# Score products of the first block: two of 128 rows in place of three of 64

## Chip, core and metric

The kernel is one program on one core of a Trainium2 chip. The metric is the device time of one execution in microseconds (us); the time before is the median of three executions.

## What is computed

Two transformer blocks follow each other. The change is in the attention of the first. Its 528 tokens (16 meta tokens and 512 of the input) are projected to q, k and v for 4 heads; each head has two maps (q and k of 64 columns each), and the output uses the difference of the two softmaxes:

```python
q = apply_rope(q.transpose(0, 2, 3, 1, 4), cos, sin)
k = apply_rope(k.transpose(0, 2, 3, 1, 4), cos, sin)
def one_block(qi):
    s = jnp.einsum('bhiqd,bhikd->bhiqk', qi, k,
                   preferred_element_type=jnp.float32) * scale
    ...
    p = jax.nn.softmax(s, axis=-1)
    a = p[:, :, 0] - lam * p[:, :, 1]
    return jnp.einsum('bhqk,bhkv->bhqv', a, v32)
o = rms_norm(o, subln_g) * (1.0 - lam_init)
h = h + jnp.einsum('blm,md->bld', mixed, w_out[l])
h = h + expert_choice_ffn(rms_norm(h, ffn_norm_g[l]), w_router[l], ...)
```

A gated convolution runs beside the attention; a routed feed-forward layer with 16 experts and the second block (mLSTM, then latent attention) follow.

## The kernel before

Every float32 operand of a product is kept as two parts in fp32r, a rounded one (high) and the rest (low); `K.split` makes them with one ScalarE copy (line 191, or 194 with a factor) and one VectorE subtraction (192, 195). A product of two such operands is three products that add up in PSUM: high by high, low by high, high by low (`TRIPLES`). `K.acc` issues them, so nearly all matmuls stand at line 198.

The first block first normalizes and transposes the tokens (`hT`). `gen_qk` then makes q or k of a pair of heads: 24 products into one of two PSUM buffers `P` for each half of the tokens, a copy to `qraw` (ScalarE, 415), the rotation (VectorE 416, a transfer that swaps rows, GpSimd 420, VectorE 421) into `t1`, of which there is one buffer, and the split into q or k. Rows 0 to 63 of q and k hold map 0 of a head, rows 64 to 127 map 1.

`gen_attn` takes a head in five token tiles, the one of 16 tokens first. For each tile and map, six products (two halves of the keys, three each) of 64 rows fill a PSUM buffer `S`; VectorE takes the maximum (484), ScalarE the exponential with its sum (486). Reciprocal, scaling and the difference of the maps follow (490 to 493); TensorE transposes the result one tile later (466), and a split writes `aT`. The columns of the 16 meta tokens are gathered in `am` and split into `aM`. At the end of a head `o`, also one of the two `S` buffers, collects 12 products with `v_sb` and 3 with the 16 meta tokens for each half; square, mean, root and scaling (516 to 531) finish it.

Heads 0 and 1 get q and k first. Then `interleave` alternates the four heads with `gen_qk` of heads 2 and 3, v of heads 2 and 3, and the convolution, by estimated costs that each piece yields. The order of the instructions on each engine is fixed when the program is built, and each engine works through its own in that order. Then the buffers are given up and `route` loads the tokens again and starts the output projection.

Of the kernel before, what the change touches and what calls it, by code (L numbers as in the profile page):

```python
# [8 lines left out]
F32 = mybir.dt.float32  # L9
F32R = mybir.dt.float32r  # L10
BF16 = mybir.dt.bfloat16
I32 = mybir.dt.int32
AF = mybir.ActivationFunctionType
OP = mybir.AluOpType
# [4 lines left out]
L = 528  # L19
# [6 lines left out]
TRIPLES = ((0, 0), (1, 0), (0, 1))  # L26
# [275 lines left out]
def block1(K):  # L302
# [21 lines left out]

    mixed = Halves([K.t(pa, [128, 4, L], F32, f"mx{i}") for i in range(2)])
    hT = [Halves([K.t(pa, [128, 4, L], F32R, f"h{i}{j}") for j in range(2)]) for i in range(2)]
    v_sb = [K.t(pr, [128, 5, 512], F32R, f"v{i}") for i in range(2)]


    xin = tc.tile_pool(name="xin", bufs=1)  # L330
# [17 lines left out]
    def values(pair, w, t):  # L348
        m, c0 = XT[t]
        o = K.t(ps, [128, 512], F32, "P", 2)  # L350
        s = slice(pair * 256, pair * 256 + 256)
        if m < 128:

            K.acc(o[:48, :256], [(mT[:, k], w[b][:, k, :]) for k in range(8) for b in range(2)])
            y = K.t(pr, [16, 256], F32, "vm")
            nc.scalar.activation(y, o[32:48, :256], AF.Copy)
            nc.vector.tensor_add(y, y, o[:16, :256])
            K.split(v_sb[0][:m, t, s], v_sb[1][:m, t, s], y)
            return
        K.acc(o[:m, :256], [(hT[a][:, k, c0:c0 + m], w[b][:, k, :]) for k in range(8) for a, b in TRIPLES])  # L360
        K.split(v_sb[0][:m, t, s], v_sb[1][:m, t, s], o[:m, :256])
# [4 lines left out]
    for t in (0, 1, 4, 2, 3):  # L366
        m, c0 = XT[t]
# [23 lines left out]
    p = p_b1.__enter__()  # L391

    HALF = [slice(0, 264), slice(264, 528)]
    qk = {(w_, 0): [K.t(p, [128, L], F32R, f"{w_}{i}", 3) for i in range(2)] for w_ in "qk"}

    def proj_T(w, j, put):

# [9 lines left out]
    def gen_qk(pair, which):  # L407
        w = K.w_get()
        for j in range(2):
            raw = K.t(p, [128, L], F32, "qraw", 2)  # L410
            sw = K.t(p, [128, L], F32, "sw", 2)
            t1 = K.t(p, [128, L], F32, "t1")

            def put(cs, o):
                nc.scalar.activation(raw[:, cs], o, AF.Copy)  # L415
                nc.vector.tensor_mul(t1[:, cs], raw[:, cs], rope[:, 0, cs])
            yield from proj_T(w, j, put)
            for b in range(4):
                nc.sync.dma_start(sw[32 * b:32 * b + 32], raw[32 * (b ^ 1):32 * (b ^ 1) + 32])
            nc.gpsimd.tensor_tensor(sw, sw, rope[:, 1], op=OP.mult)  # L420
            nc.vector.tensor_add(t1, t1, sw)
            if (which, 2 * pair + j) not in qk:
                qk[which, 2 * pair + j] = [K.t(p, [128, L], F32R, f"{which}{i}", 3) for i in range(2)]
            hl = qk[which, 2 * pair + j]
            K.split(hl[0], hl[1], t1, 0.125 if which == "q" else None)

    def gen_v(pair):
        w = K.w_get()
# [4 lines left out]
    def gen_conv(pair):  # L433
        ccs, us = [], []
        w = K.w_get()
        for j in range(2):
            c = K.t(p, [128, L], F32, "cc", 2)
            yield from proj_T(w, j, lambda cs, o: nc.scalar.activation(c[:, cs], o, AF.Copy))
            ccs.append(c)
        w = K.w_get()  # L440
        for j in range(2):
            u = K.t(p, [128, L + 2], F32, "u", 2)
            nc.gpsimd.memset(u[:, 0:1], 0.0)
            nc.gpsimd.memset(u[:, L + 1:L + 2], 0.0)
            cv = ccs[j]
            yield from proj_T(w, j, lambda cs, o: nc.vector.tensor_mul(u[:, cs.start + 1:cs.stop + 1], o, cv[:, cs]))
            wj = K.v("cw").rearrange("p (j c) -> p c j", j=3)[:, 2 * pair + j]
            nc.scalar.activation(cv, u[:, 0:L], AF.Copy, scale=wj[:, 0:1])
            nc.vector.scalar_tensor_tensor(cv, u[:, 1:L + 1], wj[:, 1:2], cv, op0=OP.mult, op1=OP.add)
            nc.vector.scalar_tensor_tensor(cv, u[:, 2:L + 2], wj[:, 2:3], cv, op0=OP.mult, op1=OP.add)  # L450
        w = K.w_get()
        for j in range(2):
            yield from proj_T(w, j, lambda cs, o: nc.vector.tensor_mul(mixed[:, 4 + 2 * pair + j, cs], o,
                                                                       ccs[j][:, cs]))

    def gen_attn(h):
        q, k = qk["q", h], qk["k", h]
        aT = [K.t(p, [128, 4, L], F32R, f"aT{i}") for i in range(2)]
        aM = [K.t(p, [16, L], F32R, f"aM{i}") for i in range(2)]
        am = K.t(p, [128, 4, 16], F32, "am")  # L460

        def trans(a, t):
            m, c0 = XT[t]
            pt = K.t(ps, [128, 4, 128], F32, "T", 2)
            for kt in range(4):
                nc.tensor.transpose(pt[:, kt, :m], a[:m, XT[kt][1]:XT[kt][1] + 128], ident[:m, :m])
            K.split(aT[0][:, :, c0:c0 + m], aT[1][:, :, c0:c0 + m], pt[:, :, :m])
            if t == 4:
                pt = K.t(ps, [128, 4, 128], F32, "T", 2)
                nc.tensor.transpose(pt[:16, 0, :16], a[:16, 0:16], ident[:16, :16])  # L470
                K.split(aM[0][:, 0:16], aM[1][:, 0:16], pt[:16, 0, :16])

        pend = None
        for t in (4, 0, 1, 2, 3):
            m, c0 = XT[t]
            mx = K.t(p, [128, 2], F32, "mx", 3)
            sm = K.t(p, [128, 2], F32, "sm", 3)
            es = []
            for i in range(2):
                r = slice(64 * i, 64 * i + 64)  # L480
                s = K.t(ps, [128, 2, 512], F32, "S", 2)
                for hf, cs in enumerate(HALF):
                    K.acc(s[:m, hf, :264], [(q[a][r, c0:c0 + m], k[b][r, cs]) for a, b in TRIPLES])
                nc.vector.reduce_max(mx[:m, i:i + 1], s[:m, :, :264], axis=AX.XY, negate=True)
                e = K.t(p, [128, L], F32, f"e{i}", 2)
                nc.scalar.activation(v2(e[:m]), s[:m, :, :264], AF.Exp, bias=mx[:m, i:i + 1], accum_out=sm[:m, i:i + 1])
                es.append(e)
                yield 700
            rs = K.t(p, [128, 2], F32, "rs", 3)
            nc.vector.reciprocal(rs[:m], sm[:m])  # L490
            nc.scalar.activation(es[0][:m], es[0][:m], AF.Copy, scale=rs[:m, 0:1])
            nc.vector.tensor_mul(rs[:m, 1:2], rs[:m, 1:2], nlam[:m])
            nc.vector.scalar_tensor_tensor(es[0][:m], es[1][:m], rs[:m, 1:2], es[0][:m], op0=OP.mult, op1=OP.add)
            if t < 4:
                nc.gpsimd.tensor_copy(am[:, t], es[0][:, 0:16])
            if pend is not None:
                trans(*pend)
                yield 545
            pend = es[0], t
        yield 0  # L500
        trans(*pend)
        pt = K.t(ps, [128, 4, 128], F32, "T", 2)
        for t in range(4):
            nc.tensor.transpose(pt[:16, t], am[:, t], ident)
        K.split(aM[0][:, 16:L], aM[1][:, 16:L], pt[:16].rearrange("p a b -> p (a b)"))
        yield 900
        o = K.t(ps, [128, 2, 512], F32, "S", 2)
        hs = slice(h * 128, h * 128 + 128)
        for hf, cs in enumerate(HALF):
            terms = [(v_sb[a][:, kt, hs], aT[b][:, kt, cs]) for kt in range(4) for a, b in TRIPLES]  # L510
            terms += [(v_sb[a][:16, 4, hs], aM[b][:, cs]) for a, b in TRIPLES]
            K.acc(o[:, hf, :264], terms)
            yield 1700
        ov = o[:, :, :264]
        sq = K.t(p, [128, L], F32, "sq")
        nc.scalar.activation(v2(sq[:, :]), ov, AF.Square)
        nc.vector.tensor_scalar_mul(v2(mixed[:, h]), ov, gs)
        y = K.t(p, [128, L], F32, "sw", 2)
        yield 0
        for cs in HALF:  # L520
            s = K.t(ps, [128, 512], F32, "P", 2)[:, :264]
            K.mm(s, onesd, sq[:, cs], True, True)
            nc.scalar.activation(y[:, cs], s, AF.Ln, bias=K.eps)
            nc.vector.tensor_scalar_add(sq[:, cs], s, EPS)
        nc.scalar.activation(y, y, AF.Exp, scale=-0.5)
        t = K.t(p, [128, L], F32, "t1")
        eng = nc.vector if h == 3 else nc.gpsimd
        eng.tensor_tensor(t, y, y, op=OP.mult)
        eng.tensor_tensor(t, t, sq, op=OP.mult)
        nc.vector.scalar_tensor_tensor(y, t, -3.0, y, op0=OP.add, op1=OP.mult)  # L530
        nc.vector.tensor_mul(mixed[:, h], mixed[:, h], y)
        yield 900
# [1522 lines left out]
```

## Time and profile before

| what | value |
|---|---|
| time of three executions | 2321.82, 2322.23 and 2324.29 us, median 2322.23 us |
| profiled execution | 2327.35 us, of which 2325.6 us from its first to its last instruction |
| mean granted TensorE clock | 0.984 of full speed |
| TensorE matmuls busy | 2228.5 us (96%) |
| VectorE busy | 1764.5 us (76%) |
| ScalarE busy | 1456.4 us (63%) |
| GpSimd busy | 233.5 us (10%) |

The profiled execution is 5 us above the median. Busy TensorE time includes the end of each matmul, which overlaps the next; how fast the engine goes is read from the distance of two starts. The score products (`S<-k,q` in a row: tile written, then tiles read) run from 67.9 to 225.5 us of the span.

### The profile page before, as it was taken

Reading aid. Unit: us, or ns where it says so; the run is one execution under the profiler, and the core shown is the slowest. Engines: PE = TensorE matmul, PEld = TensorE weight load, DVE = VectorE, ACT = ScalarE, POOL = GpSimd, SP = SyncE. Lnnn points to the kernel's source line nnn. Section 1 sums busy time; section 2 is a strip of 40 time slices with the busy share of each in tenths; the row PEclk is TensorE's granted clock in tenths of the full one; section 3 lists DMA queues with packets and bytes.
Section 4 is the critical chain, followed back from the end, with each engine's and each line's share of the span. In section 5 each row is a group of like instructions: output and inputs, shape, how many; then the busy total and the mean of one; then the engine's idle time right before and its main releaser. Section 6 shows DMA issues by size and latency. Waiting matters only on the chain.

```text
span 2325.6 us, 33331 instructions
## 1 busy us (share of the span) xinstructions
PE 2228.5 (96%) x12407; PEld 1663.0 (72%) x12407; DVE 1764.5 (76%) x2599; ACT 1456.4 (63%) x2167; POOL 233.5 (10%) x246
## 2 busy tenths in 40 slices
PE   7999897999999999999999999899999999899999
PEld 6899894565555555555555555688888899777779
DVE  5766566898888888888888899867665746676762
ACT  4555344877777777777777788745453624555651
POOL 2111252000000000000000010420000000010000
PEclk9999997999999999999999999999999999989999
DMA  5311767999999999999999899442332233211122
GB/s 170 92 55 38 274 218 282 381 373 365 377 370 372 366 362 374 369 375 368 370 361 371 300 368 387 152 157 75 100 91 73 82 119 113 65 47 61 50 91 73
DMA packets 204414, 528.55 MB, mean 227 GB/s; under 512 B 13361, under 2 KB 94895, under 8 KB 204253
## 3 DMA queue, kind: packets, MB, share of 16 engines
q1 hardware_dynamic: 196157, 507.64, 60.3%
q0 software_dynamic: 5488, 13.93, 2.4%
q10 hardware_dynamic: 2608, 4.87, 0.6%
q8 instruction: 97, 1.59, 0.3%
q14 instruction: 64, 0.52, 0.1%
HBM read 506.41 MB, written 17.82 MB: 225 GB/s over the span
## 4 chain that ended last, share of the span: by engine, by line
PE 78%; ACT 3%; DVE 2%; DMA 1%; issue 1%; POOL 0%; SPq 0%; ACTq 0%; DVEq 0%; POOLq 0%
PE P L198 23%; PE G L198 16%; PE Y L198 15%; PE U L198 14%; PE S L198 4%; PE O L198 3%; PE T L203 1%; DVE wl L165 1%; ACT wh L164 1%; ACT sa L1002 1%; PE T L1179 0%; DMA pos<-positions 0%; PE T L1853 0%; PE T L1146 0%; PE T L1077 0%
## 5 line engine op out<-in xcount | busy, mean ns | idle before, releaser
L165 DVE TENSOR_TENSOR wl<-raw,wh 128x1024 fp32r<-128x1024 f32 (+1 forms) x586 | 711.8, 1227 | 151.1 <-ACT wh L164 139.9
L164 ACT ACTIVATE wh<-raw 128x1024 fp32r<-128x1024 f32 (+1 forms) x604 | 634.0, 1055 | 284.1 <-PE O L198 66.8
L198 PE MATMUL G<-wh,xgT 128*66 128x512 f32 x1024 | 281.2, 396 | 21.5 <-ACT sa L1002 20.7
L198 PE MATMUL Y<-wh,hT 128*66 128x512 f32 x1024 | 278.3, 393 | 0.0
L198 PE MATMUL U<-wh,xgT 128*66 128x512 f32 x1024 | 277.9, 393 | 0.0
L165 DVE TENSOR_TENSOR wl<-h,wh 128x1024 fp32r<-128x1024 f32 x196 | 239.4, 1236 | 26.6 <-ACT wh L164 23.0
L198 PE MATMUL P<-hT,wh 128*128 128x512 f32 x768 | 247.9, 395 | 0.0
L164 ACT ACTIVATE wh<-h 128x1024 fp32r<-128x1024 f32 x200 | 210.5, 1059 | 57.3 <-PE G L198 22.6
L198 PEld LDWEIGHTS G<-wh,xgT 128*66 128x66 f32 x1024 | 138.4, 138 | 120.4 <-ACT sa L1002 27.0
L198 PEld LDWEIGHTS U<-wh,xgT 128*66 128x66 f32 x1024 | 139.9, 137 | 97.0
L198 PEld LDWEIGHTS Y<-wh,hT 128*66 128x66 f32 x1024 | 137.4, 137 | 90.5
L198 PEld LDWEIGHTS P<-hT,wh 128*128 128x128 f32 x768 | 143.5, 188 | 29.5
L198 PE MATMUL G<-wl,xgT 128*66 128x512 f32 x512 | 160.7, 395 | 0.0
L198 PE MATMUL U<-wl,xgT 128*66 128x512 f32 x512 | 159.9, 394 | 0.7 <-DVE wl L165 0.7
L198 PE MATMUL Y<-wl,hT 128*66 128x512 f32 x512 | 159.8, 393 | 0.0
L198 PE MATMUL P<-wh,hT 128*128 128x256 f32 (+2 forms) x712 | 148.0, 291 | 5.5 <-ACT hT L191 3.2
L198 PE MATMUL P<-hT,wl 128*128 128x512 f32 x384 | 151.3, 394 | 0.0
L198 PE MATMUL P<-h,wh 128*128 128x264 f32 x640 | 126.0, 290 | 1.6 <-ACT qraw L415 1.0
L165 DVE TENSOR_TENSOR wl<-mx,wh 128x1024 fp32r<-128x1024 f32 x96 | 116.8, 1228 | 13.9 <-ACT wh L164 12.1
L198 PEld LDWEIGHTS P<-wh,hT 128*128 128x128 f32 x712 | 117.1, 191 | 7.4 <-ACT hT L191 3.9
L164 ACT ACTIVATE wh<-mx 128x1024 fp32r<-128x1024 f32 x96 | 101.2, 1059 | 27.5 <-PE Y L198 9.6
L198 PE MATMUL P<-wl,hT 128*128 128x256 f32 (+2 forms) x408 | 117.0, 289 | 0.0
(644 smaller groups left out, 3897.3 us busy)
## 6 DMA issues: line engine op xcount, KB each, us to landing
raw<-w_gate SPq DMA_DIRECT2D x82, 1024.0 KB, 7.3
raw<-w_down SPq DMA_DIRECT2D x80, 1024.0 KB, 9.1
raw<-w_up SPq DMA_DIRECT2D x76, 1024.0 KB, 7.1
h<-w_up SPq DMA_DIRECT2D x35, 1024.0 KB, 7.0
h<-w_down SPq DMA_DIRECT2D x32, 1024.0 KB, 8.8
h<-w_gate SPq DMA_DIRECT2D x31, 1024.0 KB, 7.3
raw<-a_w_in SPq DMA_DIRECT2D x24, 1024.0 KB, 5.5
mx<-w_up SPq DMA_DIRECT2D x17, 1024.0 KB, 7.1
```

Of the source, the lines that this page charges most:

```text
L164: self.nc.scalar.activation(hv, v[:, r], AF.Copy)
L165: lo.tensor_tensor(lv, v[:, r], hv.bitcast(F32), op=OP.subtract)
L198: self.last_mm = self.nc.tensor.matmul(out, l, r, start=st, stop=sp)
L203: i = self.nc.tensor.transpose(out, src, ident)
L1002: silu = nc.scalar.activation(hh, g[:CAP], AF.Silu)
```

## The change

q and k of a head and map are laid out in 128 rows. For map `i`, `q[i]` holds the high part of the map's q in the map's own 64 rows and the low part in the other 64. k has four tiles: `kh0`, `kh1` hold the high part of map 0 or 1 in both halves, `kl0`, `kl1` the low part. So `q[i]` by `kh` gives high by high plus low by high, and `q[i]` by `kl` adds the rest: two products of 128 rows for each half of the keys. Low by low is added, which was left out before. The copies cost more instructions, each of 64 rows. The terms of the meta tokens in the output are stacked likewise: `aM` (high, high, low) and `v_m` (high, low, high) have 96 rows, with zeros between, and one product replaces three. The convolution's `cc` now uses the two `qraw` buffers.

```diff
+    v_m = K.t(pr, [96, 512], F32R, "v_m")
+    nc.gpsimd.memset(v_m.bitcast(F32), 0.0)
...
-            K.split(v_sb[0][:m, t, s], v_sb[1][:m, t, s], y)
+            for x in (0, 64):
+                nc.scalar.activation(v_m[x:x + 16, s], y, AF.Copy)
+            nc.vector.tensor_sub(v_m[32:48, s], y, v_m[0:16, s].bitcast(F32))
...
+    def new_q(which):
+
+        return [K.t(p, [128, L], F32R, f"{x}{i}", 3) for x in (("q",) if which == "q" else ("kh", "kl")) for i in range(2)]
...
+    aM = K.t(p, [96, L], F32R, "aM")
+    nc.gpsimd.memset(aM.bitcast(F32), 0.0)
...
-            hl = qk[which, 2 * pair + j]
-            K.split(hl[0], hl[1], t1, 0.125 if which == "q" else None)
+                qk[which, 2 * pair + j] = new_q(which)
+            d = qk[which, 2 * pair + j]
+            for i in range(2):
+                r, o = (slice(64 * x, 64 * x + 64) for x in (i, 1 - i))
+                if which == "q":
+
+                    nc.scalar.activation(d[i][r], t1[r], AF.Copy, scale=0.125)
+                    nc.vector.scalar_tensor_tensor(d[i][o], t1[r], 0.125, d[i][r].bitcast(F32), op0=OP.mult,
+                                                   op1=OP.subtract)
+                else:
+                    for x in (r, o):
+                        nc.scalar.activation(d[i][x], t1[r], AF.Copy)
+                    for x in (r, o):
+                        nc.vector.tensor_sub(d[2 + i][x], t1[r], d[i][r].bitcast(F32))
...
-            c = K.t(p, [128, L], F32, "cc", 2)
+            c = K.t(p, [128, L], F32, "qraw", 2)
...
+    def split_m(cs, src):
+
+        for x in (0, 32):
+            nc.scalar.activation(aM[x:x + 16, cs], src, AF.Copy)
+        nc.vector.tensor_sub(aM[64:80, cs], src, aM[0:16, cs].bitcast(F32))
...
-                    K.acc(s[:m, hf, :264], [(q[a][r, c0:c0 + m], k[b][r, cs]) for a, b in TRIPLES])
+                    K.acc(s[:m, hf, :264], [(q[i][:, c0:c0 + m], k[2 * x + i][:, cs]) for x in range(2)])
...
-            terms += [(v_sb[a][:16, 4, hs], aM[b][:, cs]) for a, b in TRIPLES]
+            terms += [(v_m[:, hs], aM[:, cs])]
```

Two places show how the instructions stand. The first is TensorE in the middle of head 0: one map of one token tile between the products of a projection (`k_422`, `k_423` are high and low k, `q_420`, `q_421` high and low q; `h` and `w` are tokens and weights). Before:

```order
L198 MATMUL P<-h_79,wh 128x264
L198 MATMUL S<-k_422,q_420 128x264
L198 MATMUL S<-k_422,q_421 128x264
L198 MATMUL S<-k_423,q_420 128x264
L198 MATMUL S<-k_422,q_420 128x264
L198 MATMUL S<-k_422,q_421 128x264
L198 MATMUL S<-k_423,q_420 128x264
L198 MATMUL P<-h_77,wh 128x264
```

With the change (`kh_425`, `kl_427` are high and low k of map 0, `q_423` the stacked q):

```order
L198 MATMUL P<-h_78,wh 128x264
L198 MATMUL S<-kh_425,q_423 128x264
L198 MATMUL S<-kl_427,q_423 128x264
L198 MATMUL S<-kh_425,q_423 128x264
L198 MATMUL S<-kl_427,q_423 128x264
L198 MATMUL P<-h_78,wl 128x264
```

Six products have become four, and their neighbours are still the projection's.

The second place is ScalarE where head 0 ends and head 1 begins (`e` exponentials and their scaling, `k` or `kh` the copies of heads 2 and 3, `aM` the meta tokens' columns, `sq` the square of head 0's output). Before:

```order
L191 ACTIVATE aT_723<-T 128x4x128
L191 ACTIVATE aM_725<-T 16x512
L486 ACTIVATE e_1302,sm<-S,mx 16x528
L191 ACTIVATE k_1228<-t_1136 128x528
L486 ACTIVATE e_1334,sm<-S,mx 16x528
L491 ACTIVATE e_1302<-e_1302,rs 16x528
L516 ACTIVATE sq<-S 128x528
```

With the change:

```order
L513 ACTIVATE e_1319,sm<-S,mx 16x528
L446 ACTIVATE kh_1139<-t_1019 64x528 x2
L446 ACTIVATE kh_1140<-t_1019 64x528 x2
L513 ACTIVATE e_1350,sm<-S,mx 16x528
L191 ACTIVATE aT_748<-T 128x4x128
L482 ACTIVATE aM<-T 16x512 x2
L518 ACTIVATE e_1319<-e_1319,rs 16x528
L513 ACTIVATE e_1365,sm<-S,mx 128x528
L446 ACTIVATE kh_1241<-t_1153 64x528 x2
L446 ACTIVATE kh_1242<-t_1153 64x528 x2
L543 ACTIVATE sq<-S 128x528
```

One copy stood between the exponentials of head 1's two first maps, that of head 3's k; now the four copies of head 2's k stand there, and the four of head 3's k stand ahead of the square. On TensorE, 22 of the 24 products of a v tile stood between head 0's first 12 products with the values and head 1's first scores; now all 24 stand ahead of both.

## Rows read from the trace of the kernel before

**Rows 1.** Busy time by stretch: engines, granted clock (PEclk), DMA share, GB/s.

```profile
64.00:113.40 49.40, 48.51 (x356) 42.85 (x354) 37.70 (x72) 28.45 (x63) 8.34 (x9) 0.97 0.32 92
113.40:242.00 128.60, 128.60 (x966) 117.07 (x964) 77.50 (x138) 63.91 (x127) 17.04 (x24) 1.00 0.16 50
```

**Rows 2.** Waits of TensorE from 64 to 242 us.

```profile
PE S L198 <- ACT aM L191: 0.7, 1, 0.7
PE S L198 <- ACT e L486: 0.2, 1, 0.2
```

**Rows 3.** Timeline of TensorE around a score group: start, length, instruction.

```profile
91.92 0.40 PE L198 MATMUL P<-h,wh 128*128 128x264 f32 x2
92.25 0.99 PE L198 MATMUL S<-k,q 64*128 64x264 f32 x6
93.18 0.39 PE L198 MATMUL P<-h,wl 128*128 128x264 f32 x1
93.40 0.41 PE L198 MATMUL P<-h,wh 128*128 128x264 f32 x2
```

**Rows 4.** Timeline of TensorE, a group with both maps in turn.

```profile
73.63 1.35 PE L198 MATMUL S<-k,q 64*128 64x264 f32 x12
74.91 0.51 PE L198 MATMUL P<-h,wh 128*128 128x264 f32 x2
```

**Rows 5.** Timeline of TensorE, head 1's products with the values.

```profile
144.49 0.28 PE L198 MATMUL P<-h,wl 128*128 128x264 f32 x1
144.70 0.51 PE L198 MATMUL S<-aM,v 16*128 16x264 f32 x2
145.13 0.52 PE L198 MATMUL P<-h,wh 128*128 128x264 f32 x2
```

**Rows 6.** Timeline of TensorE in the experts, transposes of 66 rows.

```profile
401.40 0.66 PE L203 MATMUL T<-ident,sa 66*128 66x66 f32 x8
401.87 1.15 PE L198 MATMUL G<-wh,xgT 128*66 128x512 f32 x4
```

**Rows 7.** VectorE by shape, 64 to 113.4 us: count, busy us, mean ns, idle.

```profile
L421 DVE TENSOR_TENSOR t<-t,sw 128x528 f32<-128x528 f32 x6 | 4.2, 702 | 1.6 <-POOL sw L420 1.5
L416 DVE TENSOR_TENSOR t<-qraw,rope 128x264 f32<-128x264 f32 x10 | 4.1, 450 | 0.1
...
L192 DVE TENSOR_TENSOR k<-t,k 128x528 fp32r<-128x528 f32 x4 | 2.8, 698 | 0.1
...
L484 DVE TENSOR_REDUCE mx<-S 16x1 f32<-16x528 f32 x4 | 2.7, 692 | 0.2 <-PE S L198 0.2
...
L195 DVE SCALAR_TENSOR_TENSOR q<-t,q 128x528 fp32r<-128x528 f32 x2 | 1.4, 704 | 0.0
```

**Rows 8.** ScalarE by shape, 64 to 113.4 us.

```profile
L486 ACT ACTIVATE e<-S,mx 16x528 f32<-16x528 f32 x4 | 2.7, 681 | 0.0
L191 ACT ACTIVATE k<-t 128x528 fp32r<-128x528 f32 x4 | 2.6, 645 | 4.8 <-DVE t L421 4.8
...
L191 ACT ACTIVATE aM<-T 16x512 fp32r<-16x512 f32 x1 | 0.6, 569 | 0.0
```

**Rows 9.** Timeline of TensorE where head 0 ends and head 1 begins.

```profile
102.04 0.89 PE L198 MATMUL S<-k,q 64*16 64x264 f32 x6
...
104.67 0.50 PE L198 MATMUL S<-aM,v 16*128 16x264 f32 x2 [0.71 <-ACT aM L191]
...
106.67 3.01 PE L198 MATMUL S<-aT,v 128*128 128x264 f32 x12
...
113.47 0.32 PE L198 MATMUL P<-wh,mT 128*48 128x256 f32 x1
```

**Rows 10.** Busy time and granted clock by stretch.

```profile
106.60:109.70 3.10, 3.10 (x14) 2.79 (x13) 2.23 (x5) 2.02 (x4) 0.00 (x0) 0.52 0.00 0
```

**Rows 11.** Timeline of SyncE after the last head.

```profile
241.98 2.31 SPq L584 DMA_DIRECT2D x<-x  x4
```

**Rows 12.** The chain that ended last, in order of time: start, us, what.

```profile
374.02 13.70 PE G L198 x48
```

More of the change, by code (lines that the diff above doesn't have):

```diff
@@ L326, in block1 @@
     hT = [Halves([K.t(pa, [128, 4, L], F32R, f"h{i}{j}") for j in range(2)]) for i in range(2)]
-    v_sb = [K.t(pr, [128, 5, 512], F32R, f"v{i}") for i in range(2)]
+    v_sb = [K.t(pr, [128, 4, 512], F32R, f"v{i}") for i in range(2)]
+    v_m = K.t(pr, [96, 512], F32R, "v_m")
+    nc.gpsimd.memset(v_m.bitcast(F32), 0.0)
     xin = tc.tile_pool(name="xin", bufs=1)
@@ L393, in block1 @@
     HALF = [slice(0, 264), slice(264, 528)]
-    qk = {(w_, 0): [K.t(p, [128, L], F32R, f"{w_}{i}", 3) for i in range(2)] for w_ in "qk"}
+    def new_q(which):
+        return [K.t(p, [128, L], F32R, f"{x}{i}", 3) for x in (("q",) if which == "q" else ("kh", "kl")) for i in range(2)]
+    qk = {(w_, 0): new_q(w_) for w_ in "qk"}
+    aM = K.t(p, [96, L], F32R, "aM")
+    nc.gpsimd.memset(aM.bitcast(F32), 0.0)
     def proj_T(w, j, put):
@@ L422, in gen_qk @@
             if (which, 2 * pair + j) not in qk:
-                qk[which, 2 * pair + j] = [K.t(p, [128, L], F32R, f"{which}{i}", 3) for i in range(2)]
-            hl = qk[which, 2 * pair + j]
-            K.split(hl[0], hl[1], t1, 0.125 if which == "q" else None)
+                qk[which, 2 * pair + j] = new_q(which)
[11 more added lines that the diff above has]
+                        nc.vector.tensor_sub(d[2 + i][x], t1[r], d[i][r].bitcast(F32))
     def gen_v(pair):
@@ L458, in gen_attn @@
         aT = [K.t(p, [128, 4, L], F32R, f"aT{i}") for i in range(2)]
-        aM = [K.t(p, [16, L], F32R, f"aM{i}") for i in range(2)]
         am = K.t(p, [128, 4, 16], F32, "am")
@@ L470, in trans @@
                 nc.tensor.transpose(pt[:16, 0, :16], a[:16, 0:16], ident[:16, :16])
-                K.split(aM[0][:, 0:16], aM[1][:, 0:16], pt[:16, 0, :16])
+                split_m(slice(0, 16), pt[:16, 0, :16])
         pend = None
@@ L479, in gen_attn @@
             for i in range(2):
-                r = slice(64 * i, 64 * i + 64)
                 s = K.t(ps, [128, 2, 512], F32, "S", 2)
                 for hf, cs in enumerate(HALF):
-                    K.acc(s[:m, hf, :264], [(q[a][r, c0:c0 + m], k[b][r, cs]) for a, b in TRIPLES])
+                    K.acc(s[:m, hf, :264], [(q[i][:, c0:c0 + m], k[2 * x + i][:, cs]) for x in range(2)])
                 nc.vector.reduce_max(mx[:m, i:i + 1], s[:m, :, :264], axis=AX.XY, negate=True)
@@ L504, in gen_attn @@
             nc.tensor.transpose(pt[:16, t], am[:, t], ident)
-        K.split(aM[0][:, 16:L], aM[1][:, 16:L], pt[:16].rearrange("p a b -> p (a b)"))
+        split_m(slice(16, L), pt[:16].rearrange("p a b -> p (a b)"))
         yield 900
```

## The prediction

> **What bounds the kernel now.** I read the busy time by stretch first. From 64 us, just before the first score, to 242 us, where the last head's output is complete, TensorE is busy 177.1 of 178 us at nearly the full granted clock [rows 1]. Its waits there come to 0.9 us [rows 2]. So this stage ends when TensorE has got through its queue, and a product less is time less, as long as the others keep up. VectorE is the next engine, and very unevenly: 37.7 of 49.4 us (76%) up to 113.4 us, while heads 2 and 3 still get q and k, but 77.5 of 128.6 us (60%) after that. ScalarE has 58% and 50% [rows 1]. The stage passes its end on: the loads of the next stage are issued at 241.98 us [rows 11], and from 374 us the chain that ended last runs through TensorE's expert products [rows 12]. I found nothing between that would not move along.
>
> **What a score costs.** Start distances say it, not lengths. Around a group of six score products [rows 3]: the second of the two P products starts about 0.12 after 91.92, at 92.04; the scores start at 92.25, the next P product at 93.18, the one after at 93.40. A product that follows its own kind takes about 0.12 us (six from 92.25 would end at 92.98). So the group pays 0.09 to get in, 0.20 within it and to get out, 0.10 on the second product after it: 0.39 us beyond its products. What differs between the neighbours is the number of rows, 64 against 128. The three products with 16 rows of meta tokens pay the same kind of price (144.49 to 144.70 to get in, then 0.43 for two and the way out) [rows 5].
>
> **What the change removes on TensorE.** With 128 rows on both sides I take the 0.39 as gone; 66 rows next to 128 show no such price: eight small transposes and the way back take 0.47 us (401.40 to 401.87) [rows 6], and the 96 rows of the meta tokens I take like these. Split at 113.4 us:
> - after it: 156 score products become 104 (52 x 0.12 = 6.3 us), 18 of the meta tokens 6 (1.5 us), and 26 score groups and 9 of the meta tokens lose 0.39 us each (13.6 us). Two groups hold both maps in turn, whose halves of the array overlap: twelve take 1.28 us (73.63 to 74.91) and not 1.46 plus the price [rows 4]; with the change eight take 0.97. They give 1.0 us less. In sum 20.4 us.
> - before it: 84 scores become 56, six become two, some 14 groups lose their price: about 9 us.
>
> So 29 to 30 us is the most that TensorE can give.
>
> A rule speaks against the change. The Trainium skill, TensorE: Matmul & The Clock Gate, Part 3, says that small products in different row groups of the array run at the same time, so 64 rows in pairs would be the cheaper form. By that rule alone 240 scores in pairs would cost 120 x 0.12 = 14.4 us and the change's 160 cost 19.2, a loss of 4.8. The kernel before pairs them in few places, and there twelve take 1.28 us, not the 0.72 of the rule, so the sum above stands.
>
> **What it adds.** Copies go by columns, not rows: a maximum over 16 rows takes 0.69 us [rows 7], so 64 rows cost as much as 128. Each k takes four ScalarE copies and four VectorE subtractions where it took one of each, each q two and two. Before 113.4 us that is for VectorE 4 x 3 x 0.698 + 2 x 0.704 = 9.8 us [rows 7], and for ScalarE 4 x 3 x 0.645 = 7.7 us [rows 8] and some more for q. `aM` adds a copy of 0.57 us a head [rows 8]. Two memsets on GpSimd, two small v copies and the shared `qraw` buffers I cost at nothing: GpSimd has 8.3 of 49.4 us to do [rows 1], the v tile of 16 tokens has other products behind it, and `cc` had two buffers too. Uncovered, they would cost under 1 us. Head 0's first score has to wait for more copies too; I cost that at nothing, since projection products stand ahead of it, and at 2.6 us (4 x 0.645) without them.
>
> **Up to 113.4 us VectorE takes the place of TensorE.** It needs 37.7 + 9.8 = 47.5 of the 49.4 us that the stretch takes now. TensorE's 9 us cannot be had; 1.9 us is the most that can, with no wait left. I expect a loss instead, where head 0 ends. Counting from the end of its first 12 products with the values, by the new order of ScalarE, TensorE and VectorE and the durations of [rows 7, 8]:
> - the first map's score of head 1 ends at 0.75, its maximum at 1.55, its exponential at 2.45 (0.68 and the sum's 0.2). One of the two S buffers holds head 0's output, so only now can the second map's score start.
> - VectorE then rotates head 2's k (two of 0.45, one of 0.70) until about 3.2. ScalarE's next four instructions are that k's copies, to 5.7; the second map's exponential waits behind them, to 6.6.
> - only then can the next score start, and the transposes' split and the two `aM` copies take ScalarE to 8.3. VectorE's four low parts, split, rotation and maximum come before its `aM` subtraction, which ends at about 10.2. The product with the meta tokens waits for it; with 12 more value products the output is complete at about 12.1.
> - the square waits for head 3's four k copies, to 14; the output's buffer is free at 15, the next scores go then and at 16.5, and the products of the 16-token v tile start at about 17.
>
> Before, it is 102.04 to 113.47, 11.4 us [rows 9]: 5.6 us less. TensorE comes to this place earlier by about 3 us (some eight groups at 0.63 would be 4.7, but VectorE is short there too). Such waits have cost clock already: from 106.6 to 109.7 the granted clock was 0.52, the 1.2 GHz level, after TensorE had waited 0.71 us at 104.67 and for a moment again, and twelve value products took 3.01 us [rows 9, 10]; in head 1's place twelve take 1.6 to 1.7. I add 1.4 us for more of that. The stretch loses 4 us; the bounds are a gain of 1.9 (VectorE without a wait) and a loss of 10 (the whole 5.6 and three such slow spells at 1.4).
>
> **After 113.4 us** VectorE has 77.5 us in what becomes some 110, 70%, so most of the 20.4 us should come. I take off 3 us: at heads 2 to 3 the norm's two products and eight scores follow each other with no projection between, and wait for the square, the copy out and an exponential (about 2 us of 0.6 to 0.9 each); the tail has less cover for `aM` (1 us). Bounds 12 to 20.4.
>
> **Sum.** 17.4 less 4 is 13.4 us. On the profiled execution: 2327.35 - 13.4 = 2313.95. That execution is 5.1 us above the median, and the difference carries over: 2322.23 - 13.4 = 2308.8, say **2309 us**.
>
> **Rivals.**
> - *All of it comes.* VectorE's queue has slack where I see none, and the first stretch gains too: 2322.2 - 26 to 30, about 2294. For it: TensorE's bound is clean over the whole stage. Against: 47.5 of 49.4 us. Chance 0.14.
> - *The price is not in the rows but in the change of tiles*, and stays: then the products alone count, 52 + 12 at 0.12 = 7.7 us after 113.4, less the same 7 us of losses: 2321.5. For it: only neighbours of unlike kind show it. Against: in [rows 6] tiles change as well, and no such price shows. Chance 0.06. The Trainium skill, TensorEngine Tiling (Array Packing), Key Properties, ties the price to the mode, that is to the rows: changing it drains TensorE, and changing the tile alone does not. No run here shows the drain itself, only its price.
> - *The chains of copies and exponentials hold all heads*, not head 0's end alone: 12 us in the late stretch against a loss of 10 in the first: 2320. For it: ScalarE and VectorE depend on each other at every tile. Against: 60% and 50% busy. Chance 0.16.
> - *Slower, by the clock.* If the waits at head 0's end let the granted clock stay at half through the first stretch, its products take twice as long: from 22 us of such products on (17.4 and the 4.6 of the bound) it is slower; 30 us would give about 2335. For it: the 3.1 us at 0.52 after waits much shorter. Against: projection products, which wait for nobody, follow. Chance 0.06.
>
> My forecast has 0.58, with 2302 to 2316 as its own range. For eight in ten: 2295 (most of the first rival) to 2320 (most of the third). A measurement of this kernel cannot tell under 0.2%, 4.6 us, from no change. Faster by more, under 2317.6: the forecast, the first rival and half of the third, 0.80; within: the other half and the second, 0.13; slower 0.07.
>
> **What would show it.** Score groups of four at 0.12 us a product with no price around them, from the timeline. VectorE over 90% busy from 64 us to head 0's end, and TensorE waiting there on ScalarE's exponentials and VectorE's `aM` by 5 to 10 us. From there to the last head's output about 111 us in place of 128.6. It would be wrong if the price stayed with 128 rows, if those waits were under 2 us or repeated at each head, or if a later stage took the gain back: the expert stage would then start less than 13 us earlier.

## The result, and the profile after

In the first comparison the changed kernel took 2302.72 us (median of four, 2300.99 to 2307.86) against 2323.26 for the kernel before (four runs): a ratio of 0.9904, 95% interval 0.9886 to 0.9923, some 20 us or 1% faster. Its profiled execution took 2307.86 us (span 2306.1). A second comparison, which stands among the experiments, gave 0.9916 (0.9895 to 0.9937). One execution of the kernel before, 2483.62 us at a mean granted clock of 0.843, is left out of the comparisons.

First the busy time by stretch, cut where head 0 is through (the first product of the 16-token v tile, here at 116.82 us); the columns are those of [rows 1].

```profile
64.00:116.60 52.60, 43.90 (x321) 40.48 (x319) 50.12 (x87) 39.23 (x82) 8.93 (x9) 0.90 0.29 85
116.60:227.45 110.85, 109.66 (x894) 106.75 (x892) 77.31 (x137) 63.71 (x130) 15.84 (x24) 1.00 0.18 58
100.00:110.00 10.00, 4.44 (x18) 3.05 (x19) 9.84 (x20) 7.78 (x15) 1.22 (x1) 0.66 0.13 45
110.00:120.00 10.00, 9.56 (x62) 8.82 (x61) 8.72 (x19) 8.37 (x20) 1.95 (x3) 0.83 0.01 2
```

Up to head 0's end VectorE is now 95% busy (50.12 of 52.60) and TensorE 83%, where it was 98%; behind it TensorE is full again, and the stretch takes 110.85 us in place of 128.60. TensorE's waits from 55 to 232 us add up to 11 us, 0.9 before [rows 2]:

```profile
PE S L198 <- ACT e L513: 5.6, 4, 3.4
PE S L198 <- DVE aM L483: 2.6, 2, 2.2
PE P L198 <- ACT sq L543: 0.9, 2, 0.7
PE P L198 <- DVE sq L551: 0.8, 2, 0.6
```

A score group, on TensorE's timeline, to be read beside [rows 3], and the single product with the meta tokens, beside [rows 5]:

```profile
72.29 0.28 PE L198 MATMUL P<-h,wh 128*128 128x264 f32 x1
72.41 0.28 PE L198 MATMUL S<-kh,q 128*128 128x264 f32 x1
72.53 0.28 PE L198 MATMUL S<-kl,q 128*128 128x264 f32 x1
...
72.89 0.28 PE L198 MATMUL P<-h,wh 128*128 128x264 f32 x1
73.01 0.28 PE L198 MATMUL P<-h,wl 128*128 128x264 f32 x1
...
144.35 0.40 PE L198 MATMUL P<-h,wh 128*128 128x264 f32 x2
144.59 0.29 PE L198 MATMUL S<-aM,v_m 96*128 96x264 f32 x1
144.71 1.63 PE L198 MATMUL S<-aT,v 128*128 128x264 f32 x12
```

Every start is 0.12 us behind the one before it, into the group, in it and out of it (a row with x2 holds two starts): the price of 0.39 us is gone, for 96 rows too. Where head 0 ends (to be read beside [rows 9]):

```profile
96.29 1.71 PE L198 MATMUL S<-aT,v 128*128 128x264 f32 x12 [0.95 <-ACT e L513]
...
101.92 0.30 PE L198 MATMUL S<-kh,q 128*16 128x264 f32 x1 [3.44 <-ACT e L513]
...
106.00 0.59 PE L198 MATMUL S<-kh,q 128*128 128x264 f32 x1 [0.82 <-ACT e L513]
...
109.44 0.59 PE L198 MATMUL S<-aM,v_m 96*128 96x264 f32 x1 [2.19 <-DVE aM L483]
109.82 2.85 PE L198 MATMUL S<-aT,v 128*128 128x264 f32 x12
...
116.82 0.32 PE L198 MATMUL P<-wh,mT 128*48 128x256 f32 x1
```

From the score behind the first 12 value products (97.85) to the v tile it is 19.0 us. Before, it was 11.4 us from the first score on (102.04), which 22 projection products parted from the value products. The next twelve value products take 2.85 us again, at a granted clock of 0.50, the 1.2 GHz level.

**Where the 19.5 us between the two profiles are.** To compare traces I use marks that all kernels share: the transpose of `vrows` on TensorE, the v tile's first product, the loads `x<-x` on SyncE [rows 11], the first expert product [rows 12], 1500 us after it, and a last mark some 3 us ahead of the last instruction, which I call the end. The first row is start-up, and differs by 1.3 to 1.4 us between two profiles of one and the same kernel.

| us | before | before, 2nd | changed | changed, 2nd |
|---|---|---|---|---|
| start to `vrows` | 36.67 | 35.41 | 35.29 | 36.70 |
| to the v tile | 76.80 | 75.42 | 81.53 | 81.85 |
| to `x<-x` | 128.51 | 128.52 | 110.63 | 110.88 |
| to the first expert product | 132.04 | 131.77 | 131.76 | 131.47 |
| last stretch, from 1500 us after it to the end | 448.4 | 445.9 | 443.6 | 447.2 |

The stage, from `vrows` to `x<-x`, went from 205.3 and 203.9 us to 192.2 and 192.7: 11.2 to 13.2 us less, 17.6 to 17.9 gained behind head 0's end and 4.7 to 6.4 lost before it. What is left of the 19.5 us is start-up (1.4) and the last stretch (4.8), 1500 us later, where nothing was changed. The second pair of profiles is only 9.0 us apart, with start-up and last stretch 1.3 us each the other way. From `x<-x` to the first expert product it is 131.5 to 132.0 us in all four, so up to there the gain moves along. These are the rows that the table is worked out from, of the changed kernel:

```profile
35.29 0.27 PE L96 MATMUL T<-ident,vrows 128*128 128x128 f32 x1
227.45 2.43 SPq L611 DMA_DIRECT2D x<-x  x4
359.21 12.87 PE G L198 x48
1859.40:2303.00 443.60, 420.61 (x2672) 374.44 (x2670) 270.29 (x722) 205.03 (x554) 24.95 (x22) 0.97 0.25 80
```

### The profile page after: what moved, and what is told of

Read it like the earlier page. It is cut to its first block, busy times and chain, and to the rows that moved or that the text cites. A ratio compares the mean times of both kernels' runs of the same rounds, so it can differ in the third digit from the quotient of the medians.

```text
span 2306.1 us, 33188 instructions
## 1 busy us (share of the span) xinstructions
PE 2200.1 (95%) x12311; PEld 1647.0 (71%) x12311; DVE 1774.5 (77%) x2615; ACT 1469.8 (64%) x2193; POOL 235.5 (10%) x248
## 4 chain that ended last, share of the span: by engine, by line
PE 79%; ACT 3%; DVE 2%; issue 1%; DMA 0%; POOL 0%; SPq 0%; ACTq 0%; DVEq 0%; POOLq 0%
PE P L198 24%; PE G L198 16%; PE Y L198 15%; PE U L198 14%; PE S L198 4%; PE O L198 3%; PE T L203 1%; DVE wl L165 1%; ACT wh L164 1%; ACT sa L1029 1%; PE T L1880 0%; PE T L1206 0%; PE T L1173 0%; PE T L1104 0%; DMA xg<-hn_d,idx 0%
## 5 line engine op out<-in xcount | busy, mean ns | idle before, releaser
L165 DVE TENSOR_TENSOR wl<-mx,wh 128x1024 fp32r<-128x1024 f32 x96 | 116.8, 1228 | 13.8 <-ACT wh L164 12.2
```

The costliest lines, as they stand in the source:

```text
L165: lo.tensor_tensor(lv, v[:, r], hv.bitcast(F32), op=OP.subtract)
```

## Experiments

Below, "stage" is the time from `vrows` to `x<-x`, and "waits" are TensorE's around head 0's end (95 to 118 us).

**1 and 2. Both kernels once more**

No edit in either.

> The changed kernel once more, nothing edited. In the first comparison the attention stage ended 14.5 us earlier than before (loads of the next stage issued at 227.45 against 241.98 us), while the times differ by some 20 us. Theory (the change gives what the stage shows, and the 4 to 6 us more that come later in the program are drift of later stages in one profiled execution): stage again 14 to 15 us shorter, the median 2302 to 2309, and the later drift against the kernel before is of another size in this profile, anywhere in -6 to +2 us. Rival (the change shortens the later stages too, by the other times at which their loads start): the drift is -4 to -5 us again, at the same places in the expert stage and behind it, and the median stays at 2302 to 2304.

> The kernel before once more, for a second profile. In the profiles so far the last stretch, from 1500 us after the first expert product on, has the same work and takes 448.4 us in the kernel before, 443.6 and 447.2 in two of the changed kernel, 437.3 in the one with the meta tokens alone, at a mean granted clock of 0.96, 0.97, 0.96 and 0.98. Theory (that stretch changes from execution to execution with the clock, not with the kernel): it takes another time here, between 437 and 450, while the attention stage ends within 1.5 us of 242. Rival (the length belongs to the kernel, by the time at which the stretch begins): 448 to 449 again.

The changed kernel: ratio 0.9916 (0.9895 to 0.9937), stage 192.7 us, the last stretch 447.2. The kernel before: stage 203.9 us, `x<-x` at 239.35, the last stretch 445.9. So the stage gains 11 to 13 us, less than the 14.5 that I had read off one pair of `x<-x` rows: 1.3 us of that were start-up, and in the second profile of the kernel before the clock did not fall at head 0's end, which makes its first part 1.4 us shorter. The last stretch has another length in each profile. The same 20 us of it, from 1660 us behind the first expert product, in the kernel before, in the one with the meta tokens alone, and in the masked kernel with cover (both below):

```profile
2034.00:2054.00 20.00, 18.87 (x74) 14.04 (x75) 13.53 (x49) 8.76 (x29) 0.00 (x0) 0.74 0.00 1
```

```profile
2033.50:2053.50 20.00, 18.87 (x110) 15.79 (x110) 17.47 (x58) 13.96 (x45) 0.00 (x0) 1.00 0.11 31
```

```profile
2019.80:2039.80 20.00, 18.87 (x110) 15.87 (x110) 17.45 (x57) 14.08 (x46) 0.00 (x0) 1.00 0.12 31
```

TensorE is busy equally long, and gets 74 products done at a granted clock of 0.74, 110 at 1.00. Over all 13 profiles the last stretch takes 437 to 439 us in four and 444 to 448 in nine; in these 20 us the granted clock is 1.00 in the four and 0.74 in the nine. Two kernels have two profiles each, all four long, so the profiles do not show that executions of one kernel differ. The times do: five of the changed kernel's ten lie at 2301 to 2303 us, five at 2308 to 2313. They also speak for kernels that differ in the odds. By its two profiles a short last stretch would put the kernel before at some 2313 to 2318 us (an estimate); of its 38 executions in the comparisons one lies there (2316.94), the others at 2319 to 2331. With the meta tokens alone, and a stage that is not shorter, six of seven take 2315.43 to 2318.39, among them the profiled one, whose last stretch is short. What in a kernel moves the odds is open.

**3. Meta tokens alone**

The kernel before, with only this of the change:

```
-            terms += [(v_sb[a][:16, 4, hs], aM[b][:, cs]) for a, b in TRIPLES]
+            terms += [(v_m[:, hs], aM[:, cs])]
```

> The kernel before with the meta-token part of the change alone: one product of 96 rows in place of three of 16. Theory: 8 products with 6 x 0.12 us less than before after head 0's end (1.5 us) and three groups' price there (9 x 0.39 is the upper end, 3.5 us, the products of a head being in two places), nothing at head 0's end, where aM is waited for a little longer: stage end 237 to 240.5, time 2317 to 2321. Rival (the aM copies, one more a head, are waited for at each head): no gain or a loss, stage end 241.5 or later.

The stage did not get shorter: 206.6 us, `x<-x` at 241.92. Yet the ratio is 0.9965 (0.9947 to 0.9984), 8 us faster, with the last stretch at 437.3. A measured gain of 8 us that is not in the stage changed: without the trace it would have been put down to the products saved. Behind head 0's end the stage did get shorter, 126.5 us in place of 128.5, as the theory wanted. What it missed is a wait on an exponential (2.1 us) at head 0's end, and the clock after it:

```profile
100.00:110.00 10.00, 7.88 (x43) 6.08 (x42) 7.24 (x14) 5.32 (x11) 1.57 (x2) 0.71 0.36 114
110.00:120.00 10.00, 10.00 (x47) 8.07 (x47) 5.12 (x11) 5.04 (x15) 2.38 (x2) 0.60 0.01 2
```

47 products in the second 10 us, against 84 in the second profile of the kernel before, where the clock stayed at 1.00: at 0.12 us each some 4.4 us, more than the 2.0 that the meta products gave behind it.

**4. Three products of 128 rows**

```
-[(q[i][:, c0:c0 + m], k[2 * x + i][:, cs]) for x in range(2)]
+[(q[i][:, c0:c0 + m], k[2 * x + i][:, cs]) for x in (0, 1, 1)]
```

> The layout of the change, but each half score takes three products of 128 rows, the low part of k being multiplied twice (so the scores count that part twice: this part of the computation is changed). It separates the price of 64 rows from the number of products. Theory (the price of about 0.39 us a group lies in going from 128 rows to 64 and back, and is gone with 128 rows): no gaps around the score groups, and against the change only the extra products cost, 52 x 0.12 = 6.3 us after head 0's end and little before it, where VectorE and ScalarE hold: stage end about 233.5, time 2308 to 2311. Rival (the gain came with the smaller number of products, the entry and exit price being that of another accumulation group): gaps stay at 0.3 to 0.4 us a group and the time is 2315 to 2323.

Stage 197.7 us, 4.9 to 5.5 more than the change, and a ratio of 0.9951 (0.9932 to 0.9970). A group of six products, and there is no price around it:

```profile
75.65 0.40 PE L198 MATMUL P<-h,wh 128*128 128x264 f32 x2
75.89 0.28 PE L198 MATMUL S<-kh,q 128*128 128x264 f32 x1
76.01 0.41 PE L198 MATMUL S<-kl,q 128*128 128x264 f32 x2
76.25 0.29 PE L198 MATMUL S<-kh,q 128*128 128x264 f32 x1
76.37 0.41 PE L198 MATMUL S<-kl,q 128*128 128x264 f32 x2
76.62 0.29 PE L198 MATMUL P<-h,wl 128*128 128x264 f32 x1
76.74 0.41 PE L198 MATMUL P<-h,wh 128*128 128x264 f32 x2
```

So the rows make the price, and the number of products is a term of its own: from the v tile to `x<-x` it is 115.0 us, 4.1 to 4.4 more than with the change. The median, 2315.39, missed the theory's 2308 to 2311 and lies at the rival's edge, but the rival's gaps are not there. The theory's time was counted from 2302.7, and by their times most of those executions had a short last stretch.

**5. Masked q**

Two q tiles of 128 rows a map, zero in the other map's rows; k split once:

```
+            if which == "k":
+                K.split(d[0], d[1], t1)
+                continue
...
-[(q[i][:, c0:c0 + m], k[2 * x + i][:, cs]) for x in range(2)]
+[(q[i][a][:, c0:c0 + m], k[b][:, cs]) for a, b in TRIPLES]
```

> q on 128 rows with zeros in the rows of the other map, k split once on 128 rows as in the kernel before, three products of 128 rows a half score: no price of 64 rows, and none of the change's extra k copies (each k one ScalarE copy and one VectorE subtraction again). Theory (the waits of TensorE at head 0's end, about 8 us of its 11, come from the k and q copies in ScalarE's and VectorE's queues): the waits on the exponentials and on aM before 117 us fall under 3 us, head 0's stretch ends 4 to 7 us earlier than with the change, the late stretch takes 6 us more for its 52 more products: stage end 226 to 230, time 2298 to 2306. Rival (the waits come from the two S buffers and from the quicker TensorE itself, whatever the copies): the waits stay at 7 us or more, stage end at 233 or later, time 2308 to 2312.

Waits 3.5 us, none on `aM`:

```profile
PE S L198 <- ACT e L515: 2.1, 1, 2.1
PE T L533 <- POOL am L524: 1.1, 1, 1.1
PE T L496 <- DVE e L522: 0.3, 1, 0.3
```

`x<-x` stands at 229.46, and the stage is 192.8 us, as with the change: its v tile comes 4.8 to 5.1 us earlier, and its third products cost 5.1 to 5.4 us behind that. The time, 2312.8 us (ratio 0.9946, 0.9929 to 0.9963), is above the forecast with a last stretch of 446. Without k copies the waits are less than half. But 19 projection products stand here between the value products and the next scores, none with the change: copies and cover are mixed up in this run. The third product by itself is not the reason: with it and all copies (run 4) the waits are 7.9 us.

**6 and 7. The copies elsewhere**

The other halves of kl on GpSimd:

```
-                    for x in (r, o):
-                        nc.vector.tensor_sub(d[2 + i][x], t1[r], d[i][r].bitcast(F32))
+                    nc.vector.tensor_sub(d[2 + i][r], t1[r], d[i][r].bitcast(F32))
+                    nc.gpsimd.tensor_tensor(d[2 + i][o], t1[r], d[i][r].bitcast(F32), op=OP.subtract)
```

> The changed kernel, but the other halves of kl are subtracted by GpSimd and not by VectorE. VectorE has 8 subtractions of 0.70 less before head 0's end (5.6 us), GpSimd as many more (about 1.2 us each, as its other instructions of 528 columns). Theory (VectorE is the engine that is short there): its share from 64 us to head 0's end falls to about 85%, the waits on aM vanish and those on the exponentials halve, stage end 2 to 4 us earlier than with the change, at 224 to 227. Rival (VectorE's instructions are stretched while GpSimd runs: one subtraction of q took 1.72 in place of 0.70 us beside a GpSimd product of 1.39): what VectorE saves it loses again, its busy time falls by under 3 us, and the stage ends at 227 to 230.

The other halves of kh and kl by DMA:

```
-                    for x in (r, o):
-                        nc.scalar.activation(d[i][x], t1[r], AF.Copy)
-                    for x in (r, o):
-                        nc.vector.tensor_sub(d[2 + i][x], t1[r], d[i][r].bitcast(F32))
+                    nc.scalar.activation(d[i][r], t1[r], AF.Copy)
+                    nc.vector.tensor_sub(d[2 + i][r], t1[r], d[i][r].bitcast(F32))
+                    nc.gpsimd.dma_start(d[i][o], d[i][r])
+                    nc.gpsimd.dma_start(d[2 + i][o], d[2 + i][r])
```

> The changed kernel, but the other halves of kh and kl are copied by DMA from GpSimd's queue and not by ScalarE and VectorE: each k costs ScalarE two copies and VectorE two subtractions of 64 rows, not four and four. Theory (the queues of ScalarE and VectorE hold head 0's end): TensorE's waits there fall from 8 us to 4 or less, the granted clock falls for a shorter time, VectorE is under 90% busy from 64 us to head 0's end, the stage ends 3 to 6 us earlier than with the change, at 222 to 226, and the time is 2299 to 2304. Rival (the waits come from the missing projections and the two S buffers): VectorE's share falls, the waits stay at 6 us or more, and the stage ends at 227 to 230 as before. A second thing that could go wrong is the DMA's own time, which is not known here: if it is above some 5 us, head 2's first scores wait for it.

With GpSimd (ratio 0.9919, 0.9903 to 0.9934) the stage got longer, 196.1 us, and the waits are 8.5. Its groups on GpSimd and VectorE from 64 to 117 us, and VectorE's same groups in the second profile of the change (count | busy us, mean ns):

```profile
L448 POOL TENSOR_TENSOR kl<-t,kh 64x528 fp32r<-64x528 f32 x8 | 13.4, 1671 | 8.2 <-ACT kh L446 7.8
L447 DVE TENSOR_TENSOR kl<-t,kh 64x528 fp32r<-64x528 f32 x8 | 8.6, 1072 | 1.6 <-ACT kh L446 1.4
L511 DVE TENSOR_REDUCE mx<-S 128x1 f32<-128x528 f32 x9 | 6.3, 698 | 0.0
L428 DVE TENSOR_TENSOR t<-qraw,rope 128x264 f32<-128x264 f32 x10 | 5.9, 632 | 1.1 <-POOL kl L448 0.9
```

```profile
L448 DVE TENSOR_TENSOR kl<-t,kh 64x528 fp32r<-64x528 f32 x16 | 13.3, 834 | 0.4 <-ACT kh L446 0.2
L511 DVE TENSOR_REDUCE mx<-S 128x1 f32<-128x528 f32 x10 | 7.0, 698 | 0.0
L428 DVE TENSOR_TENSOR t<-qraw,rope 128x264 f32<-128x264 f32 x10 | 3.9, 417 | 0.1
```

The rival's mechanism is right: VectorE's subtractions and rotations get longer, and its busy time from 64 us to the v tile falls by 1.9 us (51.49 to 49.58), where eight subtractions of 0.70 are 5.6. The stage came out worse than both had it. A subtraction on GpSimd took 1.67 us and not 1.2, and TensorE waited 1.7 us inside head 0 (55 to 95 us), at most 0.3 with the change, before it came to head 0's end; how much of the 3.4 to 3.9 us lost is waiting and how much is the clock (0.50 from 110 to 120 us) was not tried apart.

By DMA (ratio 0.9922, 0.9904 to 0.9940) VectorE's share from 64 to 97 us fell to 85% (28.07 of 33), as the theory wanted, but the waits stayed at 6.9 us, as the rival had it:

```profile
PE S L198 <- ACT e L513: 6.9, 4, 2.7
```

Its `x<-x` stands at 227.53, the stage is 190.8 us, 1.4 to 2.0 less than with the change. No copy of a k stands among the instructions right before the first two of these waits, 2.35 and 1.35 us: scores, maximum and exponential follow each other through two S buffers, with nothing else for TensorE to do. Two copies of a q do stand on ScalarE ahead of the first.

**8 and 9. The cover alone**

Two ways of counting attention, the first borrowing from head 2's end, the second from head 1's:

```
-        yield 0
+        yield {0: 3400, 2: -3400}.get(h, 0)
```

> The changed kernel, with one number in the interleaving altered: head 0's attention is counted 3400 dearer before its last transposes and head 2's as much cheaper, so that 24 projection products stand between head 0's first 12 value products and the second map's scores of head 1, and none stand at head 2's end. It asks whether what is lost at head 0's end is the missing cover alone or the k copies in ScalarE's and VectorE's queues. Theory (the copies make the wait; head 2's end has none, since all q and k are done): at head 0's end the waits fall by the 24 products, from about 7 us to 4 to 5, at head 2's end they are 1 to 3 us, and the clock falls for a shorter time: stage end 1 to 4 us earlier than with the change, at 224 to 227.5. Rival (a head's end without projections between waits as long wherever it stands): 6 to 8 us of waits appear at head 2's end, stage end 231 or later.

```
-        yield 0
+        yield {0: 3400, 1: -3400}.get(h, 0)
```

> The changed kernel with its copies, and the interleaving altered by 3400 between heads 0 and 1: 24 projection products within head 0's end and 24 at head 1's (0 and 73 before), heads 2 and 3 with 48 as with the change. Unlike the run that borrowed from head 2, no head's end is left bare. Theory (cover has its price only where there is none): waits at head 0's end 5 us as there, at head 1's under 1 us, no fall of the clock elsewhere: the value products end 189 to 191 us behind the values' row transpose, against 192.1 and 192.7 with the change. Rival (the lost time at head 0's end is the copies' and moves with them): 192 or later.

Ratios 0.9921 (0.9902 to 0.9939) and 0.9928 (0.9914 to 0.9941); stages 192.2 and 191.6 us. At head 0's end the waits came down to 5.4 and 6.2 us (the second has a wait of 0.6 on head 0's square, which falls behind 118 us in the first), about as expected. What was gained there came up where the cover was taken: at head 2's end 2.6 us (theory 1 to 3), at head 1's 2.4 (theory under 1, and 24 projection products still stand there), each with a fall of the clock:

```profile
180.00:190.00 10.00, 7.90 (x60) 7.32 (x59) 5.38 (x11) 5.62 (x12) 0.20 (x1) 0.91 0.20 71
190.00:200.00 10.00, 9.50 (x69) 8.73 (x68) 7.33 (x14) 7.01 (x17) 2.93 (x3) 0.92 0.00 1
```

(this is head 2's end in the first of the two). Both stages lie between the theory and the rival. All of k's copies are over by then, so head 2's bare end costs 2.6 us of waits without them, head 0's 7.6 to 8.4 with them. That cover of 24 products leaves no wait is refuted by head 1's end.

**10 and 11. Copies and cover together**

Masked q, and the changed kernel with DMA copies, with more cover at head 0's end:

```
-        yield 0
+        yield {0: 3400, 1: -3400}.get(h, 0)
```

> The kernel with masked q (no k copies, three products of 128 rows), and the interleaving altered: head 0's attention counted 3400 dearer before its last transposes, head 1's as much cheaper, so that 40 projection products stand within head 0's end in place of 19, and 20 in place of 44 at head 1's. With the copies gone, is the cover what is left of the wait? The waits so far from head 0's first 12 value products to its output: 7.6 us in the changed kernel (copies, no cover), 5.4 with 24 products of cover and the copies, 6.9 with the other halves by DMA and no cover, 3.5 with masked q and 19 products. Theory (copies and cover both count, and what they leave costs clock as well): waits under 1.5 us, the granted clock at 1.00 or nearly so, the stage 3 to 4 us shorter than with masked q alone and 2 to 4 us shorter than with the change: end of the value products 188 to 190 us behind the values' row transpose (192.75 with masked q, 192.1 and 192.7 with the change). Rival (the exponentials' chain through two S buffers holds it anyway): waits stay at 3 us or more and nothing is gained.

```
-        yield 0
+        yield {0: 5000, 1: -5000}.get(h, 0)
```

> The changed kernel with the other halves of kh and kl copied by DMA, and the interleaving altered by 5000 in the same way: 24 projection products within head 0's end, none at head 1's. Theory: waits at head 0's end fall from 6.9 to 3 to 4 us and the clock falls for a shorter time; at head 1's end, where head 3's k is all that is left, 2 to 4 us of waits come up: the value products end 187 to 190.5 us behind the values' row transpose (190.7 with the DMA copies alone). Rival (what one head's end gains the other loses, since the chain of score, maximum and exponential with two S buffers needs its time wherever no projections stand): 190.5 to 193.

Masked: one wait of 2.24 us, on `aM`, at head 0's end, the clock at 1.00 throughout, stage 191.9 us, 0.9 better than masked q, since head 1's end now waits 2.4 us; the theory's 188 to 190 us, and its waits under 1.5, missed. Ratio 0.9926 (0.9909 to 0.9942). DMA copies: the waits at head 0's end fell to 3.3 us and 3.5 came up at head 1's, as the theory had it:

```profile
109.61 0.39 PE L198 MATMUL S<-kh,q 128*128 128x264 f32 x1 [2.94 <-ACT e L513]
116.39 0.50 PE L198 MATMUL P<-wh,h 128*128 128x256 f32 x2 [0.34 <-DVE sq L551]
141.30 0.66 PE L494 MATMUL T<-ident,e 128*128 128x128 f32 x4 [1.46 <-DVE e L520]
144.96 0.39 PE L198 MATMUL S<-kh,q 128*128 128x264 f32 x1 [2.08 <-ACT e L513]
```

Its stage is the shortest of all, 188.2 us, 4.0 to 4.5 less than the change's and 16 to 17 less than before; the clock in the 10 us from 110 is 0.83. The ratio of 0.9916 (0.9903 to 0.9929) does not tell it from the change, since the last stretch varies by more.

## Why the prediction was right, and where it was off

- **The price of a score group.** Right: 0.12 us between all starts now (72.29 to 73.01), and with three products of 128 rows as well. The rival that gave it to the change of tiles is refuted, and the loss of 4.8 us by the rule on pairs did not come, in a kernel that seldom paired its products. Whether 64 rows in pairs throughout would be cheaper still was not tried.
- **After head 0's end.** 17.4 us were forecast, 17.6 to 17.9 came (128.51 and 128.52 to 110.63 and 110.88). The 3 us taken off for heads 2 to 3 and the tail were a little too much: TensorE's waits behind 117 us add up to 2.3 us, 1.7 in the second profile.
- **Up to head 0's end.** A loss of 4 us was forecast, 4.7 to 6.4 came; from the first value products to the v tile 19.0 us, for 17. In the forecast's terms, by the first pair of profiles: TensorE came to this place 2.8 us earlier (3 forecast) and spent 7.5 us more in it (5.6, and 1.4 for the clock). VectorE was 95% busy as said, but that it was full is not what held TensorE: with its share at 85% (DMA copies) the waits stayed at 6.9 us. The order of the waits was right, exponential, exponential, `aM`, but the first was mis-sized: the exponential waited for VectorE's maximum (at 100.31 us), which stood behind q's two low parts. Those took 2.45 us and not the 1.4 of [rows 7].
- **What makes the waits.** The step gave them to the k copies. The runs show two causes: the waits are 8.4 and 7.6 us with the copies and no cover, 6.9 with half the copies and no cover, 5.4 and 6.2 with the copies and 24 products of cover, 3.3 with half the copies and cover, 3.5 and 2.2 with no copies and 19 or 40 products. So cover of 24 products takes away 1.4 to 3.0 us, and going without the copies another 1.9 to 2.7: the 22 projection products that the new order no longer puts there weigh about as much as the copies. The walk had them missing, but named only the copies. How much of the loss is waiting and how much is the half clock behind it was not tried apart.
- **The sum.** 13.4 us in the stage; 11.2 to 13.2 measured, mean 12.2. Right in size, and in mechanism but for the cover. Two slips in the working change nothing: eight groups at 0.63 are 5.0 us, not 4.7, and the chances for "within" add up to 0.14, not 0.13.
- **The time.** 2309 us; 2302.72 and, in the second comparison, 2308.58. The step that failed is "nothing between that would not move along", with "the difference carries over": the last stretch does not move along, it has lengths of its own, 437 to 439 or 444 to 448 us. By their times the changed kernel's executions have the short one in five of ten, the kernel before's in one of 38. Part of the 20 us is this; why is open. That the second median lies at the forecast is luck: the kernel before took 2327.31 us there, some 19 more, and not 13.4.
- **Rivals.** *All of it comes* would have had no loss before head 0's end: refuted by the 4.7 to 6.4 us lost there. *All heads held*: refuted by those 2.3 us. *Slower by the clock*: the clock did fall (0.66 and 0.83 in the two stretches of 10 us from 100 us on, in the second profile 0.61 and 0.54), but projection products followed and it came back, to 1.00 from 120 us on.

## What to carry to other kernels

A group of products of few rows among products of 128 cost more here than its products (0.39 us a group of six): read such a price from start to start, ahead, within and behind, before counting instructions. When a change makes TensorE quicker, look for the place where its cover of independent products ends, and pay for the wait and for the half clock after it. Compare the changed stage between marks in the trace, and the other stages apart: here an edit whose stage did not get shorter measured 8 us faster, by a stretch 1500 us behind it.

## What the runs showed of the hardware that I had not expected

- **VectorE and GpSimd slow each other.** One of q's low parts took 1.72 us in place of 0.70 while a GpSimd product of two tiles ran (97.33 to 98.72 us). With subtractions on GpSimd, VectorE's own went from 834 to 1072 ns and its rotations from 417 to 632, while its maxima, which read one tile and that in PSUM, stayed at 698. GpSimd's own products went from 1341 to 1645 ns, by its spans, which are rough. The Trainium skill, SBUF — State Buffer, Who interferes with whom, says that a VectorE instruction with two SBUF inputs contends with a GpSimd instruction that reads SBUF, and a reduction does not. These rows agree.
- **The clock after a wait differs between executions.** A wait of 0.71 us on `aM` in the kernel before was followed by half clock from 106.6 to 109.7 us (0.52) in one profile, one of 0.72 by none in the other (1.00 in the same place, from 105.2 to 108.3), a difference of 1.4 us up to the v tile.
- **A DMA of half a k tile** (132 KB in the profile's count) landed 2.6 to 4.0 us after its issue, in the medians of the two runs that use it, soon enough not to be waited for but once in the stage (0.84 us, for head 0's kh, in the run with cover).
